# Expert bias and scatter matmuls as one-pass fp32r on high and low halves, with the gate moved to the slot's row

## The chip, the core and the metric

One core of a Trainium2 chip runs the whole program in one launch. The metric is the device time of that launch in microseconds, as a median over runs. TensorE is called PE here, its weight loader PEld, VectorE DVE, ScalarE ACT, GpSimd POOL and SyncE SP; SP issues nearly all weight transfers.

## The reference, cut to what matters

Two transformer blocks follow each other on 256 tokens of width 1024, all in fp32. The first has a gated mixer and then a mixture of 32 experts, of which each token takes 4:

```
logits = t @ w_router + b_router;  top_val, top_idx = top_k(logits, 4)
gate_w = softmax(top_val)
per expert e, on the tokens that chose it:
  gu = x_e @ w_exp_in[e] + b_exp_in[e]            # 1024 -> 2 x 1024
  g, u = min(gu[:1024], 7), clip(gu[1024:], -7, 7)
  a = g * sigmoid(1.702 g) * (u + 1)
  y = a @ w_exp_out[e] + b_exp_out[e]             # 1024 -> 1024
out[token] = sum over its 4 experts of gate_w * y
```

The second block (two layers, one with a convolution and a gated recurrence, one with attention) is not touched by the change.

## The kernel before

The program is traced in Python and a scheduler orders each engine's instructions: among those that are ready it takes the one that stands earliest in the program, and it holds back an instruction whose result has no free buffer yet. `tc.issue_after` and `keep` fix single places of that order.

The experts run one after the other, e = 0 to 31, each on 64 slots (a token that chose an expert has a rank, and the rank is its slot). The weights of one expert are six tiles of 2 MB, four of `w_exp_in` and two of `w_exp_out`, which SP loads into eight buffers in the order of use; a load waits until PE has read what lay in its buffer. After expert 19 stands a loop over experts with more than 64 tokens; with these inputs it has no turn, but every engine passes it.

One expert consists of these steps, with the lines of the kernel before:

- `spread_sel` (L892): four DVE operations write `sd`, 128 tokens by 128 columns for each half t of the tokens, which is the gate where the token's rank equals the slot and zero elsewhere (L896). PE transposes both halves into the PSUM bank `sT` (L900), and ACT copies it to `sTs` (L902).
- `expert_bias` (L765, matmul at L767): the bias row of the expert, held in the tile `bi` as four rows of 512 for each expert, is put into the two accumulators `pg` and `pu` by fp32 matmuls whose stationary operand is one column of the identity, spread to 64 columns. Each accumulator takes two matmuls, one for each half of its 128 partitions.
- The up-projection (L915): 32 fp32 matmuls of 512 columns on `pg` and as many on `pu`, 64 stationary columns wide. Two neighbours write the two partition halves of one accumulator.
- SwiGLU: DVE `gc` (L932), ACT `sg` (L934), DVE L935, `uc` (L937 and L938). PE transposes `uc` into `aT` (L943), ACT copies it (L946).
- The down-projection `py` (L951), 16 fp32 matmuls; ACT copies it to `ys` (L954).
- The scatter: for each half t of the tokens and each half j of the columns one fp32 matmul with 64 rows takes the slots of `ys` back to the tokens in a bank `pc` (L959), and DVE adds that bank to the sum `facc`, whose tile is named bcs in the trace (L964).
- Before every pair of experts `gather` (L873) makes the selection `sel` on DVE (L879) and brings the tokens of both into slots by 16 fp32 matmuls (L887).

A matmul on fp32 data is carried out as two instructions in the trace, one on `float32r` (fp32r) as one. PSUM has eight banks: four of tag "g" (`pg`, `pu`) and four of tag "b" (`sT`, `xg`, `aT`, `py`, `pc`). The scratch tiles that `tmp` hands out share eight buffers, those of `accp` five.

Ahead of expert 0 stand the router (L773 to L821) and, pinned between its steps by `keep`, the biases of experts 0 and 1 (`first_bias`, L770). Further steps hang in the middle of early experts (`mid`, L1109): `load_bo` loads the output biases on POOL's queue, `ln2_rows` fetches the rows of the next norm into `x_tm`, `out_bias` adds the gated output biases.

Of the kernel before, what the change touches and what calls it, by code (L numbers as in the profile page):

```python
# [9 lines left out]
F32 = mybir.dt.float32  # L10
# [8 lines left out]
NE = 32  # L19
# [53 lines left out]
def tile_kernel(  # L73
# [623 lines left out]
    wr = const.tile([128, 8, 32], F32, name="wr")  # L697
# [63 lines left out]
    bi = accp.tile([128, 512], F32, tag="a", name="bi")  # L761
    keep(nc.sync.dma_start(bi, b_exp_in[0].rearrange("e (q n) -> (e q) n", q=4)))
    first_acc = [(bank("pg", "g"), bank("pu", "g")) for _ in range(2)]

    def expert_bias(p, oh, q, pin=lambda i: i, halves=(0, 1)):  # L765
        for hv in halves:
            pin(T.matmul(p[64 * hv:64 * hv + 64, :], oh[:, q + hv:q + hv + 1].to_broadcast([128, 64]), bi,  # L767
                         start=True, stop=False))

    def first_bias(e, i, halves=(0, 1)):  # L770
        expert_bias(first_acc[e][i], ident[:, 4 * e:4 * e + 4], 2 * i, keep, halves)
# [55 lines left out]
    def load_bo():  # L827
        for n in range(2):
            bo.append(accp.tile([128, 512], F32, tag="a", name="bo")[0:32])
            nc.gpsimd.dma_start(bo[n], b_exp_out[0, :, 512 * n:512 * (n + 1)])  # L830
# [61 lines left out]
    def spread_sel(rank_ap, gate_ap):  # L892
        sd = tmp("sd", 256).rearrange("p (t s) -> p t s", t=2)
        for t in range(2):
            for d_ in range(2):
                V.tensor_scalar(sd[:, t, d_ * 64:(d_ + 1) * 64], slot_i, rank_ap[:, t:t + 1], gate_ap[:, t:t + 1],  # L896
                                op0=ALU.is_equal, op1=ALU.mult)
        p2_ = bank("sT")
        for t in range(2):
            T.transpose(p2_[:, t * 128:(t + 1) * 128], sd[:, t], ident)  # L900
        sT = tmp("sTs", 256)
        S.copy(sT, p2_[:, 0:256])  # L902
        return sT

    def expert(xg, a, sel_, oh, tin, tout, mid=None, acc=None, sums=None, ahead=None):
        sT = sel_()
        pg_, pu_ = acc or (bank("pg", "g"), bank("pu", "g"))
        if acc is None:
            expert_bias(pg_, oh, 0)
            expert_bias(pu_, oh, 2)  # L910
# [42 lines left out]
        ys = tmp("ys")  # L953
        S.copy(ys, py)  # L954
        for t in range(2):
            pc = []
            for j in range(2):
                p = sums[t, j] if sums else bank("pc")
                T.matmul(p, sT[64 * j:64 * j + 64, t * 128:(t + 1) * 128], ys[64 * j:64 * j + 64, :],  # L959
                         start=not sums, stop=True)  # L960
                pc.append(p)
            for j in range(0 if sums else 2):
                f = facc[:, t, j * 512:(j + 1) * 512]
                V.tensor_tensor(f, f, pc[j], op=ALU.add)  # L964
# [15 lines left out]
    for t in range(2):  # L980
        V.tensor_scalar(gw[:, t], eg[:, t], gr[:, t:t + 1], None, op0=ALU.mult)
    def facc_init():
        next(ada0, None)
        with tc.issue_after(first_sel):
            for t in range(2):
                V.tensor_scalar(facc[:, t], h1[:, t], ALPHA, None, op0=ALU.mult)
# [100 lines left out]
    def before_last():  # L1087
        ee = NE - 1
        with tc.issue_after(mark["ups"]):
            last_acc.extend([bank("pg", "g"), bank("pu", "g")])  # L1090
            for i in range(2):
                expert_bias(last_acc[i], ident[:, 4 * ee:4 * ee + 4], 2 * i)
            last_sel.append(spread_sel(rr[:, :, ee], gw[:, :, ee]))

    def pairs_of(e0, e1, xg, got=None):
        for e in range(e0, e1, 2):
            nxt = None
            for a in range(2):
                ee = e + a
                ld = w_exp(ee)  # L1100
                if got is not None:
                    w = got + [f() for f in ld[3:]]
                    got = None
                    tin, tout = w[0:4], w[4:6]
                else:
                    tin, tout = w_all(ld)
                if ee == 1:
                    xg = xg1.pop()
                mid = {0: after_first, 2: load_bo, 4: ln2_rows, 6: out_bias}.get(ee)  # L1109
                acc = first_acc[ee] if ee < 2 else last_acc if ee == NE - 1 else None  # L1110
                expert(xg, a if e else 0, last_sel.pop if ee == NE - 1 else lambda: spread_sel(rr[:, :, ee], gw[:, :, ee]),
                       ident[:, 4 * ee:4 * ee + 4], tin, tout, mid, acc, sums if ee == NE - 1 else None,
                       before_last if ee == NE - 2 else None)
# [10 lines left out]
    with tc.issue_after(mark["SP"]):  # L1124
        n_over = nc.values_load(ti[0:1, 16:17], min_val=0, max_val=15)
    with tc.For_i(0, n_over, 1) as it:
# [14 lines left out]
        V.tensor_scalar(rk, rk, cur[:, 1:2], None, op0=ALU.subtract)  # L1141
        xo = gather([rk])
        tin, tout = w_all(w_exp(eo, only2=True))
        expert(xo, 0, lambda: spread_sel(rk, gk), ohc, tin, tout)
# [501 lines left out]
```

## Time and profile before

| | us |
|---|---|
| median of 3 runs | 1941.65 (1935.75 to 1944.68) |
| the profiled execution | 1934.46 |
| its span, first to last instruction | 1932.7 |
| busy in it: PE | 1845.3 (95%) |
| busy in it: DVE / ACT / POOL | 814.0 / 556.6 / 91.7 |
| experts: first SwiGLU to last SwiGLU | 262.0 to 1206.9 |
| instructions on L767 (bias) and L959 (scatter) | 256 each |

The profiled execution is 7.2 us under the median. How to read the rows: a timeline row gives the start in us from the span's start, the time, engine, line, operation, output and input with their shapes, how many instructions were merged, and in brackets how long the engine had been idle before and what ended that. A matmul's own time overlaps the next one's, so the pace of a series is read from the starts. A window row gives a stretch, its length, and for each engine the busy time and the number of instructions, then the granted TensorE clock as a share of its full speed (1.00 is 2.4 GHz, 0.50 is 1.2 GHz), the busy share of the DMA engines and what they moved. A wait row says who waited for whom, for how long in total, how often, and the longest.

### The profile page before, as it was taken

To read this page: it belongs to the slowest core of one execution; us is meant where nothing else is said; L and a number is where in the kernel's file an instruction comes from. 1 tells how busy PE (TensorE), PEld (TensorE's weight loads), DVE (VectorE), ACT (ScalarE), POOL (GpSimd) and SP (SyncE) were. 2 spreads that over 40 slices of the span, in tenths; PEclk is the share of its full clock that TensorE was granted. 3 is DMA by queue.
4 is the path that set the end of the run, shared out by engine and by line. 5 is a ranking of instruction groups with operands and counts; after the bars stand their busy time and mean duration, and the time that the engine had idled before them with its cause. 6 is when DMAs were issued, how large, how long until landed. Compare 5 with 4: busy or idle time off the path is not lost.

```text
span 1932.7 us, 23544 instructions
## 1 busy us (share of the span) xinstructions
PE 1845.3 (95%) x9861; PEld 1130.0 (58%) x9861; DVE 814.0 (42%) x1452; ACT 556.6 (29%) x869; POOL 91.7 (5%) x106
## 2 busy tenths in 40 slices
PE   7999999999999999979999999899999998999999
PEld 6867743343334434324334433589888876678997
DVE  6755733122221222212122121667655565676555
ACT  4645310110010000000000000454544454564443
POOL 3000100000000000000000000100100011001000
PEclk9989999999999999989999999999999999999999
DMA  8667879999999999959999999674576566434452
GB/s 289 242 218 271 345 295 405 404 365 366 430 423 424 425 427 428 426 208 430 428 427 427 428 428 419 251 262 175 198 258 253 218 226 212 160 115 170 174 194 90
DMA packets 100303, 595.86 MB, mean 308 GB/s; under 512 B 7533, under 2 KB 8002, under 8 KB 75362
## 3 DMA queue, kind: packets, MB, share of 16 engines
q1 hardware_dynamic: 85874, 540.68, 69.6%
q0 software_dynamic: 14288, 53.63, 7.9%
q8 instruction: 79, 1.29, 0.3%
q14 instruction: 30, 0.25, 0.0%
q10 hardware_dynamic: 32, 0.01, 0.0%
HBM read 593.24 MB, written 1.06 MB: 307 GB/s over the span
## 4 chain that ended last, share of the span: by engine, by line
PE 79%; DVE 7%; issue 6%; DMA 5%; ACT 3%; POOL 1%; SPq 0%; DVEq 0%; POOLq 0%; ACTq 0%
PE pg L915 12%; PE py L951 12%; PE pu L915 9%; PE xg L887 3%; DMA wa<-in_ada_w_dram 3%; PE hid L271 3%; PE hid L270 3%; PE hid L269 3%; PE pc L959 3%; PE acc L254 3%; PE acc L255 3%; PE acc L256 3%; PE pu L767 2%; PE adp L628 2%; PE aT L943 1%
## 5 line engine op out<-in xcount | busy, mean ns | idle before, releaser
L199 DVE TENSOR_TENSOR wl<-w,wh 128x1024 fp32r<-128x1024 f32 x244 | 301.3, 1236 | 230.8 <-ACT wh L198 230.3
L198 ACT CAST wh<-w 128x1024 fp32r<-128x1024 f32 x244 | 255.9, 1049 | 315.8 <-PE acc L256 85.2
L915 PE MATMUL pg<-w,xg 128*64 128x512 f32 x1016 | 289.2, 602 | 0.0
L915 PE MATMUL pu<-w,xg 128*64 128x512 f32 x1016 | 286.4, 597 | 0.0
L951 PE MATMUL py<-w,aTs 128*64 128x512 f32 x1024 | 231.0, 598 | 3.0 <-ACT aTs L946 3.0
L964 DVE TENSOR_TENSOR bcs<-bcs,pc 128x512 f32<-128x512 f32 x124 | 77.0, 682 | 299.1 <-PE pc L959 299.1
L932 DVE TENSOR_SCALAR gc<-pg 128x512 f32<-128x512 f32 x32 | 22.1, 692 | 406.3 <-PE pg L915 406.3
L951 PEld LDWEIGHTS py<-w,aTs 128*64 128x64 f32 x1024 | 99.0, 137 | 123.9 <-issue 104.4
L915 PEld LDWEIGHTS pu<-w,xg 128*64 128x64 f32 x1016 | 82.6, 138 | 146.7 <-issue 146.6
L915 PEld LDWEIGHTS pg<-w,xg 128*64 128x64 f32 x1016 | 79.9, 138 | 137.3 <-issue 136.9
L270 PE MATMUL hid<-xhl,wh 128*128 128x256 f32 x512 | 145.2, 284 | 0.0
L271 PE MATMUL hid<-xhl,wl 128*128 128x256 f32 x512 | 145.1, 283 | 0.0
L269 PE MATMUL hid<-xhl,wh 128*128 128x256 f32 x512 | 145.0, 284 | 0.0
L934 ACT ACTIVATE sg<-gc 128x512 f32<-128x512 f32 x32 | 20.2, 630 | 389.1 <-DVE gc L932 389.1
L269 PEld LDWEIGHTS hid<-xhl,wh 128*128 128x128 f32 x512 | 98.2, 192 | 2.1 <-ACT xhl L1213 1.7
L270 PEld LDWEIGHTS hid<-xhl,wh 128*128 128x128 f32 x512 | 98.3, 192 | 1.4 <-issue 0.8
L271 PEld LDWEIGHTS hid<-xhl,wl 128*128 128x128 f32 x512 | 98.3, 192 | 0.8 <-issue 0.8
L254 PE MATMUL acc<-wh,hh 128*128 128x512 f32 x240 | 94.5, 395 | 0.0
L255 PE MATMUL acc<-wl,hh 128*128 128x512 f32 x240 | 93.7, 390 | 0.0
L256 PE MATMUL acc<-wh,hh 128*128 128x512 f32 x240 | 93.7, 390 | 0.0
L954 ACT COPY ys<-py 128x512 f32<-128x512 f32 x32 | 18.7, 585 | 236.9 <-PE py L951 236.9
L959 PE MATMUL pc<-ys,sTs 64*128 64x512 f32 x256 | 63.6, 615 | 19.5 <-ACT ys L954 19.5
(529 smaller groups left out, 2761.7 us busy)
## 6 DMA issues: line engine op xcount, KB each, us to landing
w<-in_w_exp_in_dram SPq DMA_DIRECT2D x125, 2048.0 KB, 13.1
w<-in_w_exp_out_dram SPq DMA_DIRECT2D x63, 2048.0 KB, 12.1
w<-in_mlp_w_dram SPq DMA_DIRECT2D x32, 2048.0 KB, 7.7
wa<-in_ada_w_dram POOLq DMA_DIRECT2D x38, 1024.0 KB, 7.4
w<-in_w_in_dram SPq DMA_DIRECT2D x9, 2048.0 KB, 10.5
w<-in_w_in_ab_dram SPq DMA_DIRECT2D x7, 2048.0 KB, 23.3
w<-in_w_qkv_dram SPq DMA_DIRECT2D x6, 2048.0 KB, 7.9
wa<-in_ada_w_dram POOLq DMA_DIRECT2D x20, 512.0 KB, 4.8
```

The costliest lines, as they stand in the source:

```text
L198: mark["S"] = S.copy(hi, src).ins
L199: mark["V"] = V.tensor_tensor(lo, src, hi.bitcast(F32), op=ALU.subtract).ins
L254: T.matmul(outs[t], hs, wh[:, j, :], start=a, stop=False)
L255: T.matmul(outs[t], hs, wl[:, j, :], start=False, stop=False)
L256: T.matmul(outs[t], ls, wh[:, j, :], start=False, stop=z)
L269: T.matmul(o, hs, xh[:, k + j, :], start=a, stop=False, skip_group_check=True)
L270: T.matmul(o, hs, xl[:, k + j, :], start=False, stop=False, skip_group_check=True)
L271: last = T.matmul(o, ls, xh[:, k + j, :], start=False, stop=z and m % 2 == 1, skip_group_check=True)
L915: up = T.matmul(p[64 * hv:64 * hv + 64, :], xg[:, 2 * i + r, a * 64:(a + 1) * 64], tin[i][:, r, b0 + hv * 512:b0 + (hv + 1) * 512], start= ...
L951: T.matmul(py[64 * j:64 * j + 64, :], aT[:, r * 128 + i * 64:r * 128 + (i + 1) * 64], tout[i][:, r, j * 512:(j + 1) * 512], start=i == 0 a ...
L959: T.matmul(p, sT[64 * j:64 * j + 64, t * 128:(t + 1) * 128], ys[64 * j:64 * j + 64, :], start=not sums, stop=True)
L964: V.tensor_tensor(f, f, pc[j], op=ALU.add)
```

## The change

It alters the bias, the scatter and the place of the gate, and frees the buffers that this needs.

- The bias table `bi` is split once into an fp32r high part and a low part (`bhl`, one ACT copy and one DVE subtraction). The stationary operand is no longer a spread column of the identity: `bias_sel` writes, with one DVE copy for each expert, a tile `be` of 128 by 256 in which the four bias rows are selected for 64 columns each. Each accumulator then takes two matmuls over all 128 partitions, one on the high part and one on the low part.
- `sd` holds only zeros and ones, in fp32r, so its DVE operations have one step less. The gate comes in as a matmul of `sd` with the token's gate, split in high and low (`gwr`), which puts the gate of each slot into two spare columns of the bank `sT`; DVE adds the two to `gs_`. These are two more matmuls of two columns for each expert and one small DVE operation.
- The copy `ys` becomes two: ACT writes `yh_`, `py` times the gate, as fp32r, and DVE writes `yl_`, `py` times the gate less `yh_`. Each of the four scatter matmuls becomes two fp32r ones, on `yh_` and `yl_`.
- Buffers: the router weight `wr` moves from a buffer of its own into a `tmp` buffer, and so does `bi`; the two halves `bhl` take two of the five `accp` buffers; the output biases `bo` move from `accp` into `x_tm`, and `out_bias` and `ln2_rows` change places (experts 4 and 6).

```diff
-    wr = const.tile([128, 8, 32], F32, name="wr")
+    wr = tmp("wr", 256).rearrange("p (k e) -> p k e", k=8)
...
-    bi = accp.tile([128, 512], F32, tag="a", name="bi")
+    bi = tmp("bi")
     keep(nc.sync.dma_start(bi, b_exp_in[0].rearrange("e (q n) -> (e q) n", q=4)))
+    bhl = [accp.tile([128, 512], F32R, tag="a", name=n) for n in ("bhl0", "bhl1")]
+    split(bhl[0], bhl[1], bi)
...
-    def expert_bias(p, oh, q, pin=lambda i: i, halves=(0, 1)):
-        for hv in halves:
-            pin(T.matmul(p[64 * hv:64 * hv + 64, :], oh[:, q + hv:q + hv + 1].to_broadcast([128, 64]), bi,
-                         start=True, stop=False))
+    def bias_sel(oh):
+        e_ = tmp("be", 256, F32R)
+        V.tensor_copy(e_.rearrange("p (q s) -> p q s", q=4), oh[:, :, None].to_broadcast([128, 4, 64]))
+        return e_
+
+    def expert_bias(p, e_, half, pin=lambda i: i):
+        for i in range(2):
+            pin(T.matmul(p, e_[:, 128 * half:128 * half + 128], bhl[i], start=i == 0, stop=False))
+
+    first_sel_b = [bias_sel(ident[:, 4 * e:4 * e + 4]) for e in range(2)]
...
-            bo.append(accp.tile([128, 512], F32, tag="a", name="bo")[0:32])
+            bo.append(x_tm[0:32, 0, 512 * n:512 * (n + 1)])
...
-        sd = tmp("sd", 256).rearrange("p (t s) -> p t s", t=2)
+        sd = tmp("sd", 256, F32R).rearrange("p (t s) -> p t s", t=2)
         for t in range(2):
             for d_ in range(2):
-                V.tensor_scalar(sd[:, t, d_ * 64:(d_ + 1) * 64], slot_i, rank_ap[:, t:t + 1], gate_ap[:, t:t + 1],
-                                op0=ALU.is_equal, op1=ALU.mult)
+                V.tensor_scalar(sd[:, t, d_ * 64:(d_ + 1) * 64], slot_i, rank_ap[:, t:t + 1], None, op0=ALU.is_equal)
         p2_ = bank("sT")
         for t in range(2):
-            T.transpose(p2_[:, t * 128:(t + 1) * 128], sd[:, t], ident)
+            T.transpose(p2_[:, t * 128:(t + 1) * 128], sd[:, t].bitcast(F32), ident)
+        for t in range(2):
+            T.matmul(p2_[:, 256:258], sd[:, t], gate_ap[:, t], start=t == 0, stop=t == 1, skip_group_check=True)
...
+        gs_ = small("gs_", 1)
+        V.tensor_reduce(gs_, p2_[:, 256:258], axis=AX.X, op=ALU.add)
...
-            expert_bias(pg_, oh, 0)
-            expert_bias(pu_, oh, 2)
+            eb = bias_sel(oh)
+            expert_bias(pg_, eb, 0)
+            expert_bias(pu_, eb, 1)
...
-        ys = tmp("ys")
-        S.copy(ys, py)
-        for t in range(2):
-            pc = []
-            for j in range(2):
-                p = sums[t, j] if sums else bank("pc")
-                T.matmul(p, sT[64 * j:64 * j + 64, t * 128:(t + 1) * 128], ys[64 * j:64 * j + 64, :],
-                         start=not sums, stop=True)
-                pc.append(p)
+        yh_, yl_ = tmp("yh_", 512, F32R), tmp("yl_", 512, F32R)
+        S.activation(yh_, py, AF.Copy, scale=gs_)
+        V.scalar_tensor_tensor(yl_, py, gs_, yh_.bitcast(F32), op0=ALU.mult, op1=ALU.subtract)
+        for t in range(2):
+            pc = [sums[t, j] if sums else bank("pc") for j in range(2)]
+            for i, y_ in enumerate((yh_, yl_)):
+                for j in range(2):
+                    T.matmul(pc[j], sT[64 * j:64 * j + 64, t * 128:(t + 1) * 128], y_[64 * j:64 * j + 64, :],
+                             start=i == 0 and not sums, stop=i == 1)
...
+    gwr = const.tile([128, 2, 32, 2], F32R, name="gwr")
+    split(gwr[:, :, :, 0], gwr[:, :, :, 1], gw)
...
-                mid = {0: after_first, 2: load_bo, 4: ln2_rows, 6: out_bias}.get(ee)
+                mid = {0: after_first, 2: load_bo, 4: out_bias, 6: ln2_rows}.get(ee)
```

## Rows read from the trace of the kernel before

**Rows 1.** Window of 40 us in the expert stage, columns as explained above
```profile
560.00:600.00 40.00, 39.06 (x193) 16.20 (x192) 9.18 (x20) 3.62 (x7) 0.00 (x0) 1.00 1.00 423
```

**Rows 2.** Waits of PE: the only wait on a DMA, total us, times, longest
```profile
PE adp L628 <- DMA wa<-in_ada_w_dram: 11.6, 7, 2.8
```

**Rows 3.** Timeline of SP's queue: start, us, line, transfer; two experts apart
```profile
554.75 13.87 SPq L135 DMA_DIRECT2D w<-in_w_exp_in_dram  x4
...
613.87 13.87 SPq L135 DMA_DIRECT2D w<-in_w_exp_in_dram  x4
```

**Rows 4.** Weight tiles, us to landing: window 540:600, then 1100:1160
```profile
DMA to landing us min/median/max: 10.8/10.8/10.8
...
DMA to landing us min/median/max: 21.2/21.2/21.2
```

**Rows 5.** Timeline of one expert's end: start, us, engine, line, operation, idle before
```profile
604.91 0.69 DVE L932 TENSOR_SCALAR gc<-pg 128x512 f32<-128x512 f32 x1 [14.74 <-PE pg L915]
...
607.63 0.69 DVE L938 SCALAR_TENSOR_TENSOR uc<-uc,sg 128x512 f32<-128x512 f32 x1
...
607.65 1.07 PE L767 MATMUL pu<-bi,ident 128*64 128x512 f32 x2 [0.21 <-DVE uc L937]
...
608.24 0.98 DVE L896 TENSOR_SCALAR sd<-slot_i,rr,gw 128x64 f32<-128x64 f32 x4
...
608.65 0.75 PE L943 MATMUL aT<-ident,uc 128*128 128x128 f32 x4
...
610.08 7.19 PE L951 MATMUL py<-w,aTs 128*64 128x512 f32 x32
...
617.36 0.58 ACT L954 COPY ys<-py 128x512 f32<-128x512 f32 x1 [7.34 <-PE py L951]
...
618.00 1.99 PE L959 MATMUL pc<-ys,sTs 64*128 64x512 f32 x8 [0.73 <-ACT ys L954]
...
619.16 2.48 DVE L964 TENSOR_TENSOR bcs<-bcs,pc 128x512 f32<-128x512 f32 x4 [9.94 <-PE pc L959]
...
619.92 0.44 PE L900 MATMUL sT<-ident,sd 128*128 128x128 f32 x2
```

**Rows 6.** Timeline of an expert with no bias matmul in its end
```profile
809.92 0.69 DVE L932 TENSOR_SCALAR gc<-pg 128x512 f32<-128x512 f32 x1 [10.93 <-PE pg L915]
...
813.39 0.75 PE L943 MATMUL aT<-ident,uc 128*128 128x128 f32 x4 [1.79 <-DVE uc L938]
...
822.05 0.58 ACT L954 COPY ys<-py 128x512 f32<-128x512 f32 x1 [7.24 <-PE py L951]
```

**Rows 7.** Timeline of PE: two one-pass fp32r matmuls of 512 columns in a row
```profile
224.21 0.39 PE L256 MATMUL wo<-wh,xhl 128*128 128x512 f32 x1
...
224.44 0.39 PE L254 MATMUL wo<-wh,xhl 128*128 128x512 f32 x1
```

**Rows 8.** Timeline of PE: the rank matmuls, fp32r with few columns, and the gather
```profile
244.03 0.27 PE L814 MATMUL rank<-M,uor 128*128 128x64 f32 x1 [0.65 <-DVE M L804]
...
244.35 0.26 PE L817 MATMUL rank<-M,uor 128*128 128x32 f32 x1
...
245.64 3.95 PE L887 MATMUL xg<-sel,h 128*128 128x64 f32 x32
```

**Rows 9.** Windows of 1 us around the router, columns as in rows 1
```profile
242.00:243.00 1.00, 1.00 (x4) 0.00 (x0) 0.96 (x8) 0.46 (x2) 0.14 (x1) 0.50 0.92 279
...
244.00:245.00 1.00, 0.97 (x6) 0.71 (x8) 0.35 (x3) 0.00 (x0) 0.00 (x0) 1.00 0.50 201
```

**Rows 10.** Timeline behind the overflow loop: first DVE work, first up-projection matmul
```profile
862.85 0.98 DVE L896 TENSOR_SCALAR sd<-slot_i,rr,gw 128x64 f32<-128x64 f32 x4 [5.42 <-DMA w<-in_w_exp_in_dram]
...
867.79 0.95 PE L915 MATMUL pg<-w,xg 128*64 128x512 f32 x1
```

**Rows 11.** Timelines of SP and PE: the router weight's load and first use
```profile
22.99 1.16 SPq L699 DMA_DIRECT2D wr<-in_w_router_dram  x1
...
113.84 3.62 PE L703 MATMUL lgb<-wr,vT 128*128 128x32 f32 x16
```

More of the change, by code (lines that the diff above doesn't have):

```diff
@@ L760, in tile_kernel, with first_bias @@
     V.tensor_copy(onr, ones)
-    bi = accp.tile([128, 512], F32, tag="a", name="bi")
+    bi = tmp("bi")
     keep(nc.sync.dma_start(bi, b_exp_in[0].rearrange("e (q n) -> (e q) n", q=4)))
+    bhl = [accp.tile([128, 512], F32R, tag="a", name=n) for n in ("bhl0", "bhl1")]
+    split(bhl[0], bhl[1], bi)
     first_acc = [(bank("pg", "g"), bank("pu", "g")) for _ in range(2)]
-    def expert_bias(p, oh, q, pin=lambda i: i, halves=(0, 1)):
-        for hv in halves:
-            pin(T.matmul(p[64 * hv:64 * hv + 64, :], oh[:, q + hv:q + hv + 1].to_broadcast([128, 64]), bi,
-                         start=True, stop=False))
-    def first_bias(e, i, halves=(0, 1)):
-        expert_bias(first_acc[e][i], ident[:, 4 * e:4 * e + 4], 2 * i, keep, halves)
+    def bias_sel(oh):
[6 more added lines that the diff above has]
+    first_sel_b = [bias_sel(ident[:, 4 * e:4 * e + 4]) for e in range(2)]
+    def first_bias(e, i):
+        expert_bias(first_acc[e][i], first_sel_b[e], i, keep)
     pl = bank("lg")
@@ L892, in spread_sel @@
     def spread_sel(rank_ap, gate_ap):
-        sd = tmp("sd", 256).rearrange("p (t s) -> p t s", t=2)
+        sd = tmp("sd", 256, F32R).rearrange("p (t s) -> p t s", t=2)
         for t in range(2):
             for d_ in range(2):
-                V.tensor_scalar(sd[:, t, d_ * 64:(d_ + 1) * 64], slot_i, rank_ap[:, t:t + 1], gate_ap[:, t:t + 1],
-                                op0=ALU.is_equal, op1=ALU.mult)
+                V.tensor_scalar(sd[:, t, d_ * 64:(d_ + 1) * 64], slot_i, rank_ap[:, t:t + 1], None, op0=ALU.is_equal)
         p2_ = bank("sT")
         for t in range(2):
-            T.transpose(p2_[:, t * 128:(t + 1) * 128], sd[:, t], ident)
-        sT = tmp("sTs", 256)
+            T.transpose(p2_[:, t * 128:(t + 1) * 128], sd[:, t].bitcast(F32), ident)
+        for t in range(2):
+            T.matmul(p2_[:, 256:258], sd[:, t], gate_ap[:, t], start=t == 0, stop=t == 1, skip_group_check=True)
+        sT = tmp("sTs", 256, F32R)
         S.copy(sT, p2_[:, 0:256])
-        return sT
+        gs_ = small("gs_", 1)
+        V.tensor_reduce(gs_, p2_[:, 256:258], axis=AX.X, op=ALU.add)
+        return sT, gs_
     def expert(xg, a, sel_, oh, tin, tout, mid=None, acc=None, sums=None, ahead=None):
-        sT = sel_()
+        sT, gs_ = sel_()
         pg_, pu_ = acc or (bank("pg", "g"), bank("pu", "g"))
         if acc is None:
-            expert_bias(pg_, oh, 0)
-            expert_bias(pu_, oh, 2)
+            eb = bias_sel(oh)
+            expert_bias(pg_, eb, 0)
+            expert_bias(pu_, eb, 1)
         for i in range(4):
@@ L1090, in before_last @@
             last_acc.extend([bank("pg", "g"), bank("pu", "g")])
+            eb = bias_sel(ident[:, 4 * ee:4 * ee + 4])
             for i in range(2):
-                expert_bias(last_acc[i], ident[:, 4 * ee:4 * ee + 4], 2 * i)
-            last_sel.append(spread_sel(rr[:, :, ee], gw[:, :, ee]))
+                expert_bias(last_acc[i], eb, i)
+            last_sel.append(spread_sel(rr[:, :, ee], gwr[:, :, ee]))
     def pairs_of(e0, e1, xg, got=None):
@@ L1108, in pairs_of @@
                     xg = xg1.pop()
-                mid = {0: after_first, 2: load_bo, 4: ln2_rows, 6: out_bias}.get(ee)
+                mid = {0: after_first, 2: load_bo, 4: out_bias, 6: ln2_rows}.get(ee)
                 acc = first_acc[ee] if ee < 2 else last_acc if ee == NE - 1 else None
-                expert(xg, a if e else 0, last_sel.pop if ee == NE - 1 else lambda: spread_sel(rr[:, :, ee], gw[:, :, ee]),
+                expert(xg, a if e else 0, last_sel.pop if ee == NE - 1 else lambda: spread_sel(rr[:, :, ee], gwr[:, :, ee]),
                        ident[:, 4 * ee:4 * ee + 4], tin, tout, mid, acc, sums if ee == NE - 1 else None,
@@ L1125, in tile_kernel @@
         n_over = nc.values_load(ti[0:1, 16:17], min_val=0, max_val=15)
+    gkr = const.tile([128, 2, 2], F32R, name="gkr")
     with tc.For_i(0, n_over, 1) as it:
@@ L1141, in tile_kernel @@
         V.tensor_scalar(rk, rk, cur[:, 1:2], None, op0=ALU.subtract)
+        split(gkr[:, :, 0], gkr[:, :, 1], gk)
         xo = gather([rk])
         tin, tout = w_all(w_exp(eo, only2=True))
-        expert(xo, 0, lambda: spread_sel(rk, gk), ohc, tin, tout)
+        expert(xo, 0, lambda: spread_sel(rk, gkr), ohc, tin, tout)
     pairs_of(20, NE, xg, got)
```

## The prediction

> **What bounds the kernel now.** I looked first at whether PE or the weight stream sets the pace of the expert stage, then at what lies between the matmuls of one expert. Both PE and DMA are full there: in a window of 40 us PE is busy 39.06 us and the DMA engines all of it, at 423 GB/s [rows 1]. The waits of PE decide: the only DMA that it ever waits for is the small `wa` load of another stage, 11.6 us in 7 waits; no matmul waits for an expert's weight [rows 2]. So PE's order sets the pace. Two experts take 613.87 - 554.75 = 59.12 us [rows 3], in which twelve tiles of 2.097 MB, 25.17 MB, are loaded: 425.7 GB/s, about what the window shows as a full stream, a tile every 4.93 us. A saving in PE is therefore paid out of the stream's lead. A buffer is used again eight tiles later, 8 x 4.93 = 39.4 us; the tile lands 10.8 us after its issue in the first part and 21.2 us in the second [rows 4], which leaves 28 and 18 us. A saving of 0.3 us in each of 32 experts is 10 us and fits. DMA is no cap here, and no help either.
>
> In one expert's end [rows 5] PE stands in two chains. Up to the start of `py` it is the chain over DVE and ACT: `gc` 604.91, `uc` ending at 608.32, `aT` 608.65, `py` 610.08. Behind `py`, whose end I call P (610.08 + 7.19 = 617.27), it is: ACT's copy `ys` at P + 0.09, scatter at P + 0.73, first DVE addition at P + 1.89, and the transposes `sT` at P + 2.65, right behind the end of that first addition, which frees their PSUM bank. The next up-projection follows `sT`. In every second expert the gather stands in this place, behind the same release. Work removed in these stretches counts only as far as it holds a chain up.
>
> **The bias.** Old: four fp32 matmuls, two halves at a time, 256 instructions for 32 experts. New: four fp32r matmuls of 512 columns at a pace of 224.44 - 224.21 = 0.23 us [rows 7], so 0.92 us of PE work, and half as many instructions. Most of the old work is already hidden: it fills PE's wait for `uc`. An expert with no bias in its end shows what is not: from `gc` to `ys` it takes 822.05 - 809.92 = 12.13 us [rows 6] against 617.36 - 604.91 = 12.45 [rows 5]. The difference of 0.32 is mostly that `aT` comes 0.33 us after `uc` instead of 0.06, because the matmul of 607.65 is in its way. That 0.32 is all that the bias can give back; 28 of 32 experts have it (the first two biases stand ahead of expert 0, the next two after the loop stand outside an end): -9.0 us.
>
> The new bias needs the tile `be` first, so it can't run two experts ahead any more. `be` is a DVE copy of 256 columns; the trace has none, and the nearest rows are the `sd` operations, 0.98 for four of 64 columns [rows 5], so 0.25 to 0.98. DVE is idle behind `sd` until the additions, which hides it. The four bias matmuls then have PE's waits behind `py`: of the 2.65 us from P to `sT`, scatter will take about 0.9 (below), which leaves 1.7 for 0.92. Bounds: 0 (all in waits) to 0.92 (all in the way). I take 0.05 for each expert, half of one matmul in the way in every second case: +1.5 us. The upper end is a rival below.
>
> **The scatter.** Old: `ys` copied in 0.58, then 8 instructions in 1.99 [rows 5]. New: `yh_` on ACT about 0.6, ending at P + 0.69; then `yl_` on DVE, which reads `yh_` and so stands behind it, 0.69 as `uc` [rows 5], ending near P + 1.42; its first matmul starts at P + 1.47 and, at 0.39 for one of 512 columns [rows 7], ends at P + 1.86; the first addition follows at about P + 1.94. It was P + 1.89. So half of the scatter's PE time goes, and the chain that frees the bank gets 0.05 longer: the saving on PE lands in the wait. Bounds: -0.05 (a shorter copy) to +0.5 (DVE not free when `yh_` is done). I take +0.05, 32 times: +1.6 us.
>
> **The gate.** `sd` loses one of its two steps; DVE isn't late there, so nothing. The two gate matmuls stand on PE between `sT` and the up-projection, where nothing is waited for. The nearest rows are the four fp32r rank matmuls of 32 columns and more: 244.35 - 244.03 over three steps, 0.107 us each [rows 8]. So 0.21 for each expert; bounds 0 (if they fall into a wait) and 0.44 (as the two transposes, 0.44 [rows 5]). 32 times 0.21 is +6.8 us. The Trainium skill, "TensorE: Matmul & The Clock Gate", section "Back-to-back issue gap", has some 60 cycles of TensorE for any matmul of up to 64 columns, 25 ns; by it the two cost 0.05 and the sum falls by about 5 us. The rank rows are four times slower than that, and I go by them. `gs_` on DVE comes after the additions and is first needed at the next P, some 20 us later: nothing.
>
> **Once-only places.** After the loop nothing is under way, and biases of experts 20 and 21 stand ahead of the up-projection: first DVE work 862.85, first up matmul 867.79, 4.94 us [rows 10]. New: `sd` 0.9, `be` 0.4, four bias matmuls at 0.46 (twice 0.23, since PE stood before) 1.84, `sT` 0.5, together 3.6: -1.3 us (0 to -2.5).
>
> Around the router the old bias matmuls fill PE's waits. PE's granted clock is 0.50 while they run and 1.00 from 244 on [rows 9], just ahead of the gather, 3.95 us [rows 8]. With half as much fill, PE stands idle longer, and the rise can come later. If the gather ran wholly at 0.50 it would take 3.95 us more; I take +2, bounds 0 and +5. `split` of `bi` (two operations) and two `be` stand on DVE and ACT while `w_out`'s matmuls run; nothing.
>
> `wr` was loaded at 22.99 and first used at 113.84 by matmuls that took 3.62 us [rows 11]. In a `tmp` buffer its load waits for the attention's scratch, so it moves behind other weight loads on SP, whose order it can hold up; what waits for it is that matmul group, and the rest of PE behind it. Bounds: -3.6 (the group moves into a wait) to +10.8 (PE stands for a landing as long as a queued tile's [rows 4]). I take 0, because its result is not needed until the router, 120 us later. `load_bo` now waits on POOL until expert 1 has left `x_tm`; behind it there are constants that no expert waits for. `out_bias` and `ln2_rows` only change places. In the overflow loop nothing runs.
>
> **Sum**, against the profiled execution of 1934.46: -9.0 + 1.5 + 1.6 + 6.8 - 1.3 + 2 = +1.6, so 1936.1. It stands 7.2 us under the median of the runs, on which the forecast goes: 1941.65 + 1.6, about **1943 us**. My reading is that about half of the PE work is taken out of bias and scatter, and nearly all of that was hidden.
>
> **Rivals.** *The gate and bias matmuls all fall into waits*: -9.0 + 1.6 - 2.5 and nothing else, so -10, 1932. For it: 1.7 us of waits behind P. Against: the gate matmuls read `sd` right behind its transposes, after the last wait. By the skill's 25 ns it would be nearly this, 1934.
>
> *The selector comes late* (the slower side): DVE writes `be` only when a scratch buffer is free and after `sel` and `sd`. One expert now draws nine `tmp` tiles where it drew seven, out of the same eight buffers. If `be` is written only behind `yl_` or the additions, the bias matmuls miss the waits and stand ahead of the up-projection, 0.92 in full; and where `sd` and `be` are written just before `yl_`, they push it and the bank's release by up to 0.5. It decides from the point at which `be` ends later than about P + 1.7 (`sT` less the bias's own time). For it: `sd` is written only after `uc` though its inputs are long there [rows 5], which looks like a want of buffers. Against: four buffers fall free (`gc`, `sg`, `uc`, `aT`'s source) before P. In half of the experts it gives 14 x 0.87 = +12, 1955; in all +24, 1967.
>
> *The fp32r halves don't run side by side*: the two 64-row halves of the old scatter do, 8 instructions in 1.99 [rows 5]. If the new ones don't, scatter is 8 x 0.23 = 1.84, the room for the bias shrinks to 0.8 and each expert pays about 0.15 more: +5, 1948.
>
> **How the numbers follow.** Forecast and its once-only spread, 0.55; halves not side by side, 0.05 (both within 0.5% of 1941.65, which is 9.7 us and about what a measurement of this kernel can tell from no change); all in waits, 0.13; selector late, 0.22; an unplanned stall at `wr` or the router at its upper bound, 0.05. So faster 0.13, same 0.60, slower 0.27. The likeliest one's own range is 1936 to 1950. The range of 8 in 10 takes in the mechanism of the first rival to its end with some spread and the second up to most of the experts: 1930 to 1965.
>
> **What would show it.** Right: `aT` starts within 0.1 us of `uc`'s end; first DVE addition at P + 1.9 to 2.0; the period of two experts within 0.3 us of 59.12; the bias matmuls lie between P and the next `sT`. Wrong on the gate: the up-projection starts less than 0.1 us or more than 0.3 us later behind `sT`. Wrong on the selector: a DVE copy `be` that ends behind the first addition, and a PE wait for it. Wrong on the start: a clock of 0.50 beyond the gather. What would upset it most is an order on DVE or PE in which `yl_` stands behind other work.

## The result and the profile after

| | before | after |
|---|---|---|
| median of 4 runs each, us | 1941.67 | 2096.88 (2091.77 to 2100.77) |
| ratio, with its 95% interval | | 1.0803 (1.078 to 1.0825) |
| span of the profiled execution | 1932.7 | 2091.8 |
| granted clock, mean of the span | 0.985 | 0.941 |
| busy: PE | 1845.3 (95%) | 1888.3 (90%) |

The change makes the kernel 8% slower, outside the predicted range. PE is busy for longer than before, 1888.3 us, and yet for a smaller share of the span. The same 40 us window as in [rows 1], columns as there:

```profile
560.00:600.00 40.00, 35.18 (x162) 15.59 (x156) 8.67 (x21) 3.97 (x7) 0.00 (x0) 0.91 0.82 342
```

PE lost 3.9 us of busy time, the granted clock fell from 1.00 to 0.91, and the weight stream from 423 to 342 GB/s: the DMA engines now have time to spare. What PE waits for (who waits for whom, total us, times, longest):

```profile
PE aT L955 <- DVE uc L950: 50.5, 28, 2.1
PE sT L907 <- DVE sd L904: 38.4, 16, 9.2
PE py L963 <- ACT aTs L958: 20.3, 30, 0.7
PE xg L895 <- DVE sel L887: 12.0, 14, 0.9
PE adp L628 <- DMA wa<-in_ada_w_dram: 10.9, 7, 2.4
```

The only wait on a DMA is that of [rows 2]. New are the waits for `sel` and `sd`, and those for `uc` and `aTs` have grown (5.6 and 3.0 us before), because the old bias had filled them: in [rows 5] with the matmul of 607.65, and between `aT` and `py` with this one, of the kernel before:

```profile
609.33 1.07 PE L767 MATMUL pu<-bi,ident 128*64 128x512 f32 x2
```

Of the 38.4 us for `sd`, two waits stand apart from the ends of the experts: 9.2 us once behind expert 1, where the tables of the overflow loop (`later_consts`) stand ahead of `sd` on DVE, and 8.2 at the overflow loop, where the kernel before waits 7.7 as well. The timeline of PE over the ends of two experts, columns as in [rows 5]:

```profile
564.44 0.75 PE L955 MATMUL aT<-ident,uc 128*128 128x128 f32 x4 [1.85 <-DVE uc L950]
565.86 8.78 PE L963 MATMUL py<-w,aTs 128*64 128x512 f32 x32 [0.68 <-ACT aTs L958]
...
577.50 1.10 PE L895 MATMUL xg<-sel,h 128*128 128x128 f32 x4 [0.31 <-DVE bcs L976]
579.46 5.10 PE L895 MATMUL xg<-sel,h 128*128 128x128 f32 x28 [0.85 <-DVE sel L887]
584.40 0.38 PE L907 MATMUL sT<-ident,sd 128*128 128x128 f32 x2
584.53 0.36 PE L909 MATMUL sT<-gwr,sd 128*128 128x2 f32 x2
584.76 0.71 PE L774 MATMUL pg<-bhl,be 128*128 128x512 f32 x2
...
585.86 1.08 PE L927 MATMUL pg<-w,xg 128*64 128x512 f32 x4
...
603.09 7.09 PE L963 MATMUL py<-w,aTs 128*64 128x512 f32 x32 [0.68 <-ACT aTs L958]
...
614.98 0.48 PE L907 MATMUL sT<-ident,sd 128*128 128x128 f32 x1 [1.63 <-DVE sd L904]
...
615.54 1.20 PE L774 MATMUL pg<-bhl,be 128*128 128x512 f32 x2
...
617.52 1.98 PE L927 MATMUL pg<-w,xg 128*64 128x512 f32 x4
```

Three things are to be seen. Between the up-projection and `aT` there is a hole of 1.85 us, where [rows 5] had bias matmuls. The bias now stands in line, between `sT` and the next up-projection. And work behind a hole is slow: one `py` takes 8.78 us instead of 7.19 [rows 5], the first four up-projection matmuls behind the bias 1.98 instead of 1.08. The reason for the order is on DVE, in the first of these two ends:

```profile
575.41 0.75 DVE L967 SCALAR_TENSOR_TENSOR yl__3561<-py,gs__3486,yh__3560 128x512 fp32r<-128x512 f32 x1 [11.03 <-ACT yh__3560 L966]
576.08 0.57 DVE L887 TENSOR_SCALAR sel<-slot_i,rr 128x64 f32<-128x64 f32 x3
576.76 2.48 DVE L976 TENSOR_TENSOR bcs<-bcs,pc 128x512 f32<-128x512 f32 x4
...
579.32 0.73 DVE L904 TENSOR_SCALAR sd<-slot_i,rr 128x64 fp32r<-128x64 f32 x4
579.97 0.28 DVE L769 CAST be<-ident 128x256 fp32r<-128x256 f32 x1
```

`sel`, `sd` and `be` depend on nothing that is late, and DVE stood idle for 11.03 us ahead of `yl_`. Before, `sd` was written right behind `uc` [rows 5]; now all three stand behind `yl_`, and `sd`, `be` and the last of the four `sel` operations (579.16) behind the additions too.

The granted clock, in windows of 2 us at the holes of the first of these experts and behind them (columns as in [rows 9]):

```profile
564.00:566.00 2.00, 0.89 (x6) 0.70 (x8) 0.38 (x1) 0.58 (x1) 0.00 (x0) 1.00 1.05 451
...
568.00:570.00 2.00, 2.00 (x6) 0.49 (x4) 0.00 (x0) 0.00 (x0) 0.00 (x0) 0.50 0.98 418
...
580.00:582.00 2.00, 2.00 (x13) 2.00 (x13) 0.26 (x2) 0.00 (x0) 0.00 (x0) 0.58 0.98 418
```

PE had the two waits ahead of the first fall, 1.85 and 0.68 us, and was then at 1.2 GHz while it had no wait at all. The last row shows the same for the gather, behind the waits of 0.79, 0.31 and 0.85 us; 0.58 is a mean, with most of the window at 1.2 GHz. The Trainium skill, "TensorE: Matmul & The Clock Gate", section "HAM oscillation — how this bites in real kernels", tells of a kernel in which each group of matmuls starts at the low clock again, because PE waits for a DMA ahead of it. The trace agrees with that pattern, though the waits here are for DVE and ACT: in windows of 40 us from 280 to 1360 the mean clock lies between 0.83 and 1.00, most often at 0.91.

Where the time went, from PE's timeline between `aT` of expert 1 and `aT` of the last expert, called the stage below: each row counts from its start to the next row's start, less the idle time in brackets, which has a line of its own. The last four columns are experiments told below.

| us | before | after | e4 | e9 | e6 | e8 |
|---|---|---|---|---|---|---|
| up-projection | 421.2 | 437.2 | 434.2 | 465.8 | 429.3 | 424.2 |
| py | 216.2 | 240.0 | 249.9 | 211.3 | 212.0 | 213.0 |
| bias | 78.6 | 44.6 | 43.3 | 35.3 | 35.4 | 35.4 |
| gather | 54.2 | 80.5 | 54.2 | 60.8 | 55.8 | 55.6 |
| scatter | 59.5 | 54.5 | 53.6 | 54.0 | 54.1 | 53.1 |
| aT, sT and gate | 31.1 | 39.3 | 35.3 | 38.5 | 36.6 | 32.9 |
| other | 8.6 | 7.7 | 7.9 | 8.5 | 8.0 | 7.9 |
| idle | 41.4 | 154.5 | 143.0 | 81.2 | 80.4 | 69.5 |
| sum | 910.9 | 1058.3 | 1021.5 | 955.4 | 911.5 | 891.6 |

The change saved 34.0 us of bias and 5.0 of scatter. It lost 113.1 us to idle time, 66.1 us because up-projection, `py` and gather take longer for the same work, and 8.2 us in `aT`, `sT` and the gate matmuls.

### The profile page after: what moved, and what is told of

Read it like the earlier page. It is cut to its first block, busy times and chain, and to the rows that moved or that the text cites. A ratio compares the mean times of both kernels' runs of the same rounds, so it can differ in the third digit from the quotient of the medians.

```text
span 2091.8 us, 23501 instructions
## 1 busy us (share of the span) xinstructions
PE 1888.3 (90%) x9797; PEld 1156.5 (55%) x9797; DVE 841.0 (40%) x1550; ACT 563.1 (27%) x873; POOL 91.6 (4%) x106
## 4 chain that ended last, share of the span: by engine, by line
PE 74%; DVE 11%; issue 6%; DMA 4%; ACT 3%; POOL 1%; SPq 0%; DVEq 0%; POOLq 0%; ACTq 0%
PE py L963 12%; PE pg L927 12%; PE pu L927 9%; PE xg L895 4%; DVE bcs L976 3%; PE hid L271 3%; DMA wa<-in_ada_w_dram 3%; PE hid L270 3%; PE hid L269 3%; PE acc L254 3%; PE acc L255 3%; PE acc L256 3%; PE adp L628 2%; PE aT L955 1%; PE pg L774 1%
## 5 line engine op out<-in xcount | busy, mean ns | idle before, releaser
L927 PE MATMUL pg<-w,xg 128*64 128x512 f32 x1016 | 277.0, 626 | 0.0
L963 PE MATMUL py<-w,aTs 128*64 128x512 f32 x1024 | 254.9, 656 | 20.3 <-ACT aTs L958 20.3
L927 PE MATMUL pu<-w,xg 128*64 128x512 f32 x1016 | 267.4, 607 | 0.0
L963 PEld LDWEIGHTS py<-w,aTs 128*64 128x64 f32 x1024 | 77.2, 149 | 177.4 <-issue 151.2
L927 PEld LDWEIGHTS pu<-w,xg 128*64 128x64 f32 x1016 | 75.8, 142 | 155.4 <-issue 155.4
L927 PEld LDWEIGHTS pg<-w,xg 128*64 128x64 f32 x1016 | 73.3, 144 | 148.1 <-issue 147.7
L895 PE MATMUL xg<-sel,h 128*128 128x128 f32 (+1 forms) x544 | 97.4, 347 | 18.0 <-DVE sel L887 12.0
L895 PEld LDWEIGHTS xg<-sel,h 128*128 128x128 f32 x544 | 88.9, 251 | 31.4 <-DVE bcs L976 15.2
```

Source lines behind the costliest of these rows:

```text
L895: pin(T.matmul(p[:, kc * 128:kc * 128 + w], h1[:, t, 256 * i + r:256 * (i + 1):2], sel[:, t, 0:w], start=t == 0, stop=t == 1))
L927: up = T.matmul(p[64 * hv:64 * hv + 64, :], xg[:, 2 * i + r, a * 64:(a + 1) * 64], tin[i][:, r, b0 + hv * 512:b0 + (hv + 1) * 512], start= ...
L963: T.matmul(py[64 * j:64 * j + 64, :], aT[:, r * 128 + i * 64:r * 128 + (i + 1) * 64], tout[i][:, r, j * 512:(j + 1) * 512], start=i == 0 a ...
```

## The experiments

Two readings were open. **Order** (theory A): `sel`, `sd` and `be` come late, so PE waits for them and the bias stands in line. **Clock** (theory B): the holes that the old bias used to fill let the clock fall, and that is most of the loss. And the first of them has two possible reasons: a want of buffers, as my rival had it, or the order in which scratch tiles are handed out.

### Each half of the change alone

e1_bias_only: bias as changed; scatter, gate and `sd` of the kernel before.

```diff
-        yh_, yl_ = tmp("yh_", 512, F32R), tmp("yl_", 512, F32R)
-        S.activation(yh_, py, AF.Copy, scale=gs_)
...
+        ys = tmp("ys")
+        S.copy(ys, py)
```

> The new bias alone: scatter, gate and sd are those of the kernel before. In the order of DVE sd stands right behind uc again, be behind the additions. Theory A (the order: the selectors stand late on DVE, so PE waits for sd and sel and the bias stands in the path) puts only the bias into the path here, 28 x 0.92 = +26 us, no wait for sd: 1960 to 1972 us. Theory B (the clock: the old bias filled the wait for uc, the hole of 1.85 us in each expert now lets the granted clock fall) has the hole in full: the clock below 0.96 and over 2010 us.

2022.31 us, ratio 1.0431 (1.0398 to 1.0463), clock 0.958. Over the band of the order theory, and what the clock theory asked for. But a wait came in that neither had priced: `be` is written only behind the additions, so PE waits for it as well. Its row among the waits of PE:

```profile
PE pg L774 <- DVE be L769: 20.9, 14, 1.5
```

And a `py` behind the hole, from its timeline:

```profile
612.54 9.92 PE L960 MATMUL py<-w,aTs 128*64 128x512 f32 x32 [0.73 <-ACT aTs L955]
```

e2_scatter_only: scatter and gate as changed; the bias of the kernel before.

```diff
-            eb = bias_sel(oh)
-            expert_bias(pg_, eb, 0)
-            expert_bias(pu_, eb, 1)
+            expert_bias(pg_, oh, 0)
+            expert_bias(pu_, oh, 2)
```

> The new scatter and gate alone: the bias is that of the kernel before and fills the wait for uc again; sel and sd stand behind yl_ on DVE. Theory A: waits for sd and sel as in the changed kernel, 1.6 to 2.8 us for two experts and nothing for the bias: 1970 to 1995 us. Theory B: the hole at uc is filled, so the clock stays at 0.98 and the time near 1950 us.

1994.9 us, ratio 1.0294 (1.0267 to 1.0321), clock 0.976. The size is what the order theory said, but the form is not: PE hardly waits for `sd` or `sel`. With the bias already in place, the next up-projection starts into the wait, and the late gather and transposes cut it up:

```profile
607.46 0.50 PE L887 MATMUL xg<-sel,h 128*128 128x128 f32 x2 [0.31 <-DVE bcs L967]
607.89 1.07 PE L918 MATMUL pg<-w,xg 128*64 128x512 f32 x2
608.89 0.50 PE L887 MATMUL xg<-sel,h 128*128 128x128 f32 x2
...
641.09 1.08 PE L918 MATMUL pg<-w,xg 128*64 128x512 f32 x4
```

Two instructions, one half of an accumulator alone, take from 607.89 to 608.89, 1.0 us; four, both halves side by side, take 0.91 (641.09 to the next row at 642.00). A pair that is torn costs nearly twice. The up-projection is 18.7 us longer here (439.9 in all) and the bias 13.6 (92.2), of 46.8 in the stage; how much of it the torn pairs alone make is not measured.

### The clock alone

```diff
         uc = tmp("uc")
+        for _ in range(7):
+            T.matmul(pg_, bhl[0][:, 0:128], bhl[0], start=True, stop=True, skip_group_check=True)
...
         aT = tmp("aTs")
+        for _ in range(2):
+            T.matmul(pg_, bhl[0][:, 0:128], bhl[0], start=True, stop=True, skip_group_check=True)
```

> The changed kernel with nine fp32r matmuls of 512 columns added in each expert, seven between the up-projection and aT and two between aT and py, into the bank pg after gc has read it; what they write is used by nobody. Buffers and the order of all other work stay. Theory A: no gain, 2095 to 2110 us. Theory B: the clock rises from 0.94 to 0.97 or more, py takes 7.1 us in every expert, the first up-projection matmuls 1.03, and the time falls by 60 us or more, to 2000 to 2035.

2076.65 us, ratio 1.0701 (1.0669 to 1.0732), clock 0.948: 20 us under the changed kernel, where the clock theory wanted 60 or more. Its step was right, its size was not. The 20 us are what is left after the fillers' own cost: in the stage `py` falls by 28 us, but the fillers add 75 us of PE time where the idle time falls by 58. `py` takes 7.09 us now; but the second hole, behind the scatter, is still there, and the clock still falls behind it:

```profile
601.64 7.09 PE L967 MATMUL py<-w,aTs 128*64 128x512 f32 x32 [0.44 <-ACT aTs L962]
...
613.53 0.47 PE L907 MATMUL sT<-ident,sd 128*128 128x128 f32 x1 [1.63 <-DVE sd L904]
...
616.07 1.98 PE L927 MATMUL pg<-w,xg 128*64 128x512 f32 x4
```

So the clock theory alone falls: even the 28 us are under half of what it wanted. The low clock is a surcharge on the holes, and the holes come from the order.

### Why the selectors are late

e4_yl_pool: `yl_` in a buffer of its own.

```diff
+    ylp = [st2.enter_context(tc.tile_pool(name="ylp", bufs=1))]
...
-        yh_, yl_ = tmp("yh_", 512, F32R), tmp("yl_", 512, F32R)
+        yh_ = tmp("yh_", 512, F32R)
+        yl_ = ylp[0].tile([128, 512], F32R, tag="yl", name="yl_")
```

> The changed kernel with yl_ in a buffer of its own; in the order of DVE sel and sd come back to their place behind uc, be stays behind the additions. Theory A: the waits of PE for sd (38 us in all) and sel (12 us) go: 2045 to 2055 us, the wait for uc and the late bias stay. Theory B: the hole at uc stays and the clock with it (0.94 to 0.95): at most 20 us less, 2075 or more.

2055.76 us, ratio 1.0611 (1.058 to 1.0642): 41 us less. That is 0.8 us above the order theory's band and 19 us under the clock theory's. DVE behind `uc`, which ends at 586.47:

```profile
586.39 0.74 DVE L904 TENSOR_SCALAR sd<-slot_i,rr 128x64 fp32r<-128x64 f32 x4
597.51 0.75 DVE L968 SCALAR_TENSOR_TENSOR yl__3708<-py,gs__3633,yh__3707 128x512 fp32r<-128x512 f32 x1 [10.38 <-ACT yh__3707 L967]
598.85 2.48 DVE L977 TENSOR_TENSOR bcs<-bcs,pc 128x512 f32<-128x512 f32 x4 [0.59 <-PE pc L973]
...
601.32 0.28 DVE L769 CAST be<-ident 128x256 fp32r<-128x256 f32 x1
```

`sd` is back behind `uc`, the waits for `sel` are gone and gather is back at 54.2 us; `be` stays late, and so does the hole at `uc`. The idle time falls by only 11.5 us, since PE now waits for `be` instead (1.3 us in after):

```profile
PE pg L774 <- DVE be L769: 20.5, 14, 1.5
```

Most of the gain is the gather, 26.3 us, which no longer has a wait for `sel` in it and the low clock behind that.

e5_reuse: two scratch tiles less in each expert, seven out of eight buffers as in the kernel before.

```diff
-        uc = tmp("uc")
+        uc = gc
...
-        aT = tmp("aTs")
+        aT = sg
```

> The changed kernel with two scratch tiles less in each expert: uc is written into gc's tile and aT into sg's, seven tiles out of eight buffers as in the kernel before. If sel, sd and be are late for want of a free buffer (my prediction's rival), they come back behind uc and the time falls by 50 us or more. If tiles are handed out in the order of the program (be stands behind sTs, sd and sel behind yl_, whatever is free), nothing changes: sel and sd behind yl_, 2085 to 2105 us.

2105.99 us in one execution: no gain. On DVE `sel` stands where the change has it:

```profile
572.19 0.75 DVE L967 SCALAR_TENSOR_TENSOR yl__3543<-py,gs__3470,yh__3542 128x512 fp32r<-128x512 f32 x1 [9.39 <-ACT yh__3542 L966]
572.86 0.57 DVE L887 TENSOR_SCALAR sel<-slot_i,rr 128x64 f32<-128x64 f32 x3
```

So it is not the number of buffers. Taken together, e4 and e5 fit one rule of the kernel's scheduler, which is read from them and not tested by itself: tiles of one pool are handed out in the order of the program. `yl_` is the first scratch tile that DVE itself writes behind `py`; `sel` and `sd`, traced after it, can't be placed ahead of it on DVE, whatever is free. The old `ys` was written by ACT and held nothing up on DVE.

Why `be` is late stays open. `yl_` is not the reason, since `be` is late in e1 too, where there is no `yl_`, and in e4. It is traced behind `sTs`, the copy of the transposed `sd`, and by the rule it would be placed only after that; but on the chip it doesn't wait for it. In after it is written at 579.97, and ACT writes `sTs` later:

```profile
585.08 0.38 ACT L911 CAST sTs<-sT 128x256 fp32r<-128x256 f32 x1
```

What is shown is that `be` is in time when it is traced earlier (e9 and e6, next).

### The same work in another order

e9_be_early: `be` of the next expert is traced ahead of `gc`, its bias matmuls behind the last up-projection matmul. e6_early: `sd` and `sel` too, by `make_sd` and `make_sel`, the DVE parts of `spread_sel` and `gather`.

```diff
         take_sum(0, last)
+        if pre:
+            pre()
         gc = tmp("gc")
...
+    def pre_of(ee):
+        def run():
+            if ee + 1 not in (20, NE - 1, NE):
+                got_early["sd", ee + 1] = make_sd(rr[:, :, ee + 1])
+            if ee and ee + 1 not in (20, NE - 1, NE):
+                be_ = bias_sel(ident[:, 4 * ee + 4:4 * ee + 8])
+                with tc.issue_after(mark["ups"]):
+                    got_early["acc", ee + 1] = (bank("pg", "g"), bank("pu", "g"))
+                    for i in range(2):
+                        expert_bias(got_early["acc", ee + 1][i], be_, i)
+            if ee % 2 == 0 and ee + 2 < NE and ee not in ():
+                got_early["sel", ee + 2] = make_sel([rr[:, :, ee + 2 + b] for b in range(2)])
...
+        return run
```

The experts at the loop and at the end keep their places.

> The changed kernel with be alone traced ahead of gc, and its bias matmuls behind the last up-projection matmul as in e6_early; sd and sel stay where the change has them, behind yl_. If the two delays add up, be is worth what e6_early gained less what e4_yl_pool gained: 149 - 41 = 108 us, so 1985 to 1995. If the holes feed each other through the clock, be alone gives less, 2010 or more. The up-projection should then start ahead of the late sT and be torn by it as in e2_scatter_only, its sum 10 us or more above e6_early's.

1989.31 us, ratio 1.0248 (1.0226 to 1.027). The two delays add up in number: 108 us for `be`, 41 for `sel` and `sd`. In kind they don't: in the change the 41 us lie in the gather and in waits, and here, against e6, in an up-projection that is torn again as expected, 465.8 us. That both come to 41 is partly luck.

> The changed kernel with sd, be and sel of the next expert traced ahead of gc in the program, and its four bias matmuls behind the last up-projection matmul; the work is the same. The hole at uc then holds 0.92 us of bias and 0.9 us of nothing; sd and sel are in time. Theory A (order alone): the kernel before plus the two gate matmuls, 1940 to 1955 us. Theory B (what is left of the hole, and 0.68 behind aT and 0.79 behind py, still lets the clock fall): clock 0.97 or less, 1960 to 1985.

1948.27 us, ratio 1.0039 (1.0016 to 1.0062), clock 0.975: 149 us of the 155 are back, with the same arithmetic, the same number of tiles and the same instructions. That is in the order theory's band. It takes in the clock as well, since the bias now fills most of the hole at `uc`. One expert's end in it, and the start of the next but one, on PE:

```profile
582.36 0.73 PE L774 MATMUL pg<-bhl,be 128*128 128x512 f32 x2
...
584.28 0.75 PE L965 MATMUL aT<-ident,uc 128*128 128x128 f32 x4 [0.72 <-DVE uc L960]
585.70 7.09 PE L973 MATMUL py<-w,aTs 128*64 128x512 f32 x32 [0.68 <-ACT aTs L968]
...
595.63 4.04 PE L899 MATMUL xg<-sel,h 128*128 128x128 f32 x32 [0.31 <-DVE bcs L986]
...
627.72 1.97 PE L935 MATMUL pg<-w,xg 128*64 128x512 f32 x4
```

DVE in the same end:

```profile
580.76 0.69 DVE L954 TENSOR_SCALAR gc<-pg 128x512 f32<-128x512 f32 x1 [9.46 <-PE pg L935]
...
593.55 0.75 DVE L977 SCALAR_TENSOR_TENSOR yl__3841<-py,gs__3756,yh__3840 128x512 fp32r<-128x512 f32 x1 [9.33 <-ACT yh__3840 L976]
594.89 2.48 DVE L986 TENSOR_TENSOR bcs<-bcs,pc 128x512 f32<-128x512 f32 x4 [0.59 <-PE pc L982]
```

And ACT's `yh_`:

```profile
592.83 0.69 ACT L976 ACTIVATE yh__3840<-py,gs__3756 128x512 fp32r<-128x512 f32 x1 [7.19 <-PE py L973]
```

The bias lies in the hole and leaves 0.72 us of it. Behind an expert without gather the clock still falls for a moment (627.72).

e7_early_fill: eight matmuls that nobody uses are put into what is left of the holes, four behind the bias, two behind `aT` and two behind `py` (the first four are shown).

```diff
+        for _ in range(4):
+            T.matmul(pg_, bhl[0][:, 0:128], bhl[0], start=True, stop=True, skip_group_check=True)
...
```

> e6_early with eight fp32r matmuls of 512 columns added in each expert, into the bank pg after gc has read it, used by nobody: four behind the bias, two behind aT, two behind py. Theory A: as e6_early or slower by what they overrun, 0 to +10 us. Theory B: clock 0.98 or more and 1940 to 1955 us, under e6_early by 10 or more.

1940.32 us, ratio 0.9998 (0.9979 to 1.0016), clock 0.98: 8 us under e6, which is the clock theory's direction, short of the 10 that it wanted. I read the 8 us as what the clock takes when the order is right, less what the fillers cost; in the stage the up-projection takes 422.3 us instead of 429.3.

### A version that beats both kernels

e8_sT_ahead: e6 with the next expert's transposes `sT` and gate matmuls behind `aT`, in PE's wait for `aTs`.

```diff
         S.copy(aT, p)
+        if nxt_sT:
+            with tc.issue_after(last.ins):
+                nxt_sT()
         py = bank("py")
```

> e6_early with the transposes sT and the gate matmuls of the next expert placed right behind aT, in PE's wait for the copy aTs; the work is the same. It takes 0.5 to 0.9 us for each expert out of the path behind the scatter (gates, transposes, the wait for the bank): 15 to 25 us under e6_early by theory A, until PE waits for weights, whose lead is 18 to 28 us. By theory B more, since the hole behind aT is filled as well: 25 to 45 under e6_early.

1926.04 us, ratio 0.9923 (0.99 to 0.9946): 0.8% faster than the kernel before, 8% faster than the change as it was made, and 22 under e6, in the band of the order theory. PE behind `aT`:

```profile
578.82 0.38 PE L915 MATMUL sT<-ident,sd 128*128 128x128 f32 x2
578.95 0.36 PE L917 MATMUL sT<-gwr,sd 128*128 128x2 f32 x2
579.65 7.09 PE L976 MATMUL py<-w,aTs 128*64 128x512 f32 x32 [0.34 <-ACT aTs L968]
```

And a row among its waits, the only one on an expert's weight:

```profile
PE pg L935 <- DMA w<-in_w_exp_in_dram: 0.2, 1, 0.2
```

That is new in this case, and it lies at the last expert (1194.30), so there the lead of the stream is used up. That a further saving in PE would be given back is an estimate; e10 and e11 show no wait for an expert's weight.

e10_router_fill puts two more matmuls ahead of each of the first four bias pairs, and e11_all_fill six more into each expert's waits; what they write is overwritten or used by nobody.

```diff
     def first_bias(e, i):
+        for _ in range(2):
+            keep(T.matmul(first_acc[e][i], first_sel_b[e][:, 0:128], bhl[0], start=True, stop=True))
         expert_bias(first_acc[e][i], first_sel_b[e], i, keep)
```

> e8_sT_ahead with two more fp32r matmuls of 512 columns ahead of each of the four first bias pairs, into the bank that the bias then overwrites; the router's waits get as much PE work as in the kernel before. If the late rise of the clock behind the router is what the start lost (gather 7.06 us instead of 3.95, the first up-projection 4.5 us late): gather near 3.95 and 3 to 5 us under e8_sT_ahead, 1921 to 1924. If the clock has another cause there: no change or +1 us.

1926.7 us, ratio 0.9927 (0.9902 to 0.9952). The step is seen, the gain is not: the first gather takes 3.87 us where e8 and the changed kernel have 7.06, but the time is that of e8, whose runs spread by 7 us and these by 12. On PE's timeline of e10:

```profile
250.12 3.87 PE L901 MATMUL xg<-sel,h 128*128 128x64 f32 x32
```

On that of the changed kernel:

```profile
244.94 7.06 PE L895 MATMUL xg<-sel,h 128*128 128x64 f32 x32
```

> e10_router_fill with six fp32r matmuls of 512 columns added in each expert, three behind the bias and three behind py, into the bank pg, used by nobody; they lie in waits. If what is left of the holes still costs clock (0.978 against 0.985 before): 4 to 10 us under e10_router_fill. If not, or if the weights now end last: within 2 us of it.

1924.36 us, ratio 0.9915 (0.9892 to 0.9937): 2.3 us under e10, between the two cases and within the spread of e10's runs. The stage takes 891.0 us against 891.6 in e8, with its idle time down from 69.5 to 25.2, 44.3 us. The bias row, in which the fillers stand, goes from 35.4 to 84.6, 49.2 us: the fillers cost more than the waits that they fill.

## Why the prediction was wrong

**The step that failed** is the one on the selector. I wrote that DVE is idle behind `sd` until the additions, "which hides it", that `sd` is not late, and that `yl_` ends near P + 1.42 with all else in its place, and priced the bias at 0.05 for each expert: I took the order of DVE from the trace of before and put the new operations into it. But the order is made anew. `yl_`, the first scratch tile that DVE writes behind `py`, puts `sel` and `sd` behind itself (41 us, e4), and `be` comes late with its bias (108 us, e9), while DVE stands idle for 11.03 us ahead of them. I named this as a rival, at 0.22, and as what would upset the forecast most; the sign that I gave for it, `be` behind the first addition, came (579.97 against 576.76). Its reason, nine tiles out of eight buffers, was wrong (e5).

**The rival's price was wrong as well**, and that is why the range didn't hold the time. It counted the bias in the path at 0.87 and closed at 1967. It left out three things that the runs show. The old bias did not only cost PE time, it ran ahead and let the next up-projection start in a wait; e9, where it does so again, is 108 us under the change. PE waits not for `be` alone (1.3 us) but for `sel` and `sd`: 12.0 + 38.4 us, of which 17.4 are the two single waits. And a hole costs more than its length, since the clock falls behind it, as the windows at `py` and gather show: up-projection, `py` and gather take 66.1 us more. I spoke of the clock at the router alone, though the trace had the warning in a number: 1.00 in [rows 1], in a stage whose holes were filled.

**Point by point**, against e6, where the selectors are in time as I assumed, though the bias lies ahead of `aT` and not behind `py`:
- PE's order sets the pace: right. No weight is waited for in after; the DMA share fell with PE. In e8, whose stage is 19.3 us shorter than before, a tile lands 28.5 us after its issue in the window 1100:1160, where it took 21.2 [rows 4], and at the last expert the lead is used up.
- The old bias gives back 0.32: right in kind, 0.38 here. From `gc` to `yh_` it takes 592.83 - 580.76 = 12.07 us, against 12.45. The new bias in waits behind P: wrong; in after it is in the path, in e6 ahead of `aT`.
- The scatter's chain: mis-sized. `yh_` takes 0.69 where I took 0.6, `yl_` 0.75 where I took 0.69, and the first addition starts at P + 2.10 (594.89 - 592.79), not P + 1.94; the gather follows at P + 2.84. That is +0.19 for each expert (P + 2.65 before) where I had +0.05, 6.1 us in all. The halves do run side by side (593.57 and 593.58), but the scatter's PE time did not fall by half: 54.1 us against 59.5, with the wait for `yl_` in it.
- The gate: 0.13 for each expert, not 0.21 (`sT` and gate 14.4 us in e6, `sT` 10.6 in before, over the 30 experts of the stage). The Trainium skill, "TensorE: Matmul & The Clock Gate", section "Back-to-back issue gap", gives 25 ns for each, or about 62 ns where instructions are not decoded in hardware, a case that I left out; for two that would be 0.05 or 0.12. The measured 0.13 is nearer the second, but it is a mean over ends of which some run at the low clock, and does not decide.
- The loop: from `sd` to the first up-projection 3.34 us in after (968.41 to 971.75), against 4.94 [rows 10]; 3.6 was forecast.
- The router: upper bound. The first gather takes 7.06 us where it took 3.95 [rows 8], and the third group of the up-projection, the first at full pace in after, starts 4.5 us later (256.04 against 251.52).

Put together with these sizes, -0.38 x 28 + 0.19 x 32 + 0.13 x 32 - 1.6 + 4.5 is +2.5 us. That this lies near my +1.6 is luck: the scatter's chain and the router were 4.5 and 2.5 us too low, the gate 2.6, the bias 3.1 and the loop 0.3 too high. e6 measured +6.2 (interval 3 to 12). In the stage alone it takes 0.6 us more than before, where these sizes without the router's give about -2.0; what makes up the difference is not shown. So the sum was near the mark only for an order which the change did not have.

## What to carry to other kernels

When an operation is added, first ask what it does to the order, not what it costs: which queue writes its result, which pool that comes from, and what is traced behind it and must now wait for its turn. Work that looks expensive may be what fills a wait; before making it smaller, look at what else could stand there, and place the small work in the hole by hand (here: trace the next expert's selectors early, and pin its bias behind the last up-projection). A hole is to be priced with the slow matmuls that follow it.

## What had not been expected of the hardware

- Behind waits of 1.85 and 0.68 us, close together, the granted clock was 0.50 (568 to 570 in after) and `py` took 8.78 to 9.92 us instead of 7.09; not in each expert, though (603.09 in after: 7.09).
- Two matmuls that write different halves of the 128 partitions share their time only if they stand next to each other: 1.0 us for one half alone, 0.91 for both (e2). They need not belong to one accumulator: in e2 a half of `pg` starts at 609.32 and a half of `pu` at 609.33. An order that puts small matmuls between them goes with 36.5 us more of up-projection (465.8 in e9, 429.3 in e6); a part of that is the clock, 0.53 at a torn half from 609.6 to 611.5 in e9.
